# Add and layer norm: the fourth 16 rows loaded in two halves of 8, with the first store between the halves

## The chip, the cores and the metric

The kernel runs on one core of a Trainium2 chip. The metric is the time of one execution on the device, in microseconds (us).

## The reference

```python
# x, residual: (16, 1024, 512) float32; gamma, beta: 512; eps a number
z = x + residual
mean = np.mean(z, axis=-1, keepdims=True)
var  = np.var(z, axis=-1, keepdims=True)
return gamma * (z - mean) / np.sqrt(var + eps) + beta
```

There are 16,384 rows of 512 numbers. Each of the 128 partitions gets 128 rows. Whatever the kernel does, it must read 67.1 MB and write 33.6 MB.

## The kernel before

All large transfers go through one queue (the one of SP, the sync engine), in the order of a written plan. `x48+16` loads rows 48 to 63 of each partition from x, `r48+16` the same of the residual, `o0+16` stores the finished rows 0 to 15.

```python
PLAN = """
x0+8 r0+8 x8+8 r8+8 x16+16 r16+16 x32+16 r32+16
x48+16 r48+16 o0+16 r64+16 x64+16 o16+16 r80+16 x80+16
o32+16 r96+16 x96+8 x104+8 o48+16 r112+16 x112+8 x120+8
o64+16 o80+16 o96+16 o112+12 o124+4
"""
ADDS = [4, 4, 8] * 7 + [4] * 4          # rows of one add on POOL
Z_ROWS, R_ROWS = 64, 32                 # rings: rows of x (and result), of the residual
```

Before SP issues a transfer it waits for what that transfer needs, and while it waits nothing behind it in the plan is issued:

```python
    for kind, lo, n in moves:
        if kind == "x":        # the ring slot must have been stored
            while gone < len(stores) and stores[gone][0] < lo + n - Z_ROWS:
                nc.sync.wait_ge(so[gone], 16)
                gone += 1
            move(...)
        elif kind == "r":      # the ring slot must have been added
            wait_rows(s_add, "add", lo + n - R_ROWS)
            move(...)
        else:                  # the rows must be finished
            wait_rows(s_out, "out", lo + n)
            move(...)
```

So x64 waits until the store o0 has landed, r48 until 32 rows have been added, and o0 until 16 rows are finished. POOL (GpSimd) adds, ACT (ScalarE) takes the mean and the sum of squares of four rows at a time, DVE (VectorE) normalises in place:

```python
    for n in ADDS:                                    # POOL
        ...                                           # waits for the loads of these rows
        nc.gpsimd.tensor_tensor(out=z, in0=z, in1=part(rbuf, R_ROWS, lo, n), op=ALU.add
        ).then_inc(s_add, n)
    # ACT, per group of 4 rows (TURN), in a loop
            act.wait_ge(s_dve, due)
            act.wait_ge(s_add, due)
            ...
            for k in range(TURN):
                i = act.activation(out=junk_m[k][:, :], in_=zk[k], func=ACT.Identity,
                                   scale=-inv_d, accum_out=nm[j][:, k : k + 1])
            ...                                       # Square with accumulation, then Sqrt
```

## Time and profile before

| | |
|---|---|
| Time, median of the first 3 runs | 238.39 us (238.26 to 238.57) |
| Span of the profiled execution | 236.9 us |
| Bytes moved | 100.68 MB, 425 GB/s over the span |
| Busy share of the span | queue q1 99.2%, ACT 78%, DVE 75%, POOL 60% |

These lines are from the page of the kernel before: busy time of each engine, the DMA share in tenths in 40 slices of the span, and of the queues their packets, MB and the share of the time of all 16 DMA engines.

```profile
span 236.9 us, 1471 instructions
...
PE 3.7 (2%) x4; PEld 1.2 (0%) x4; DVE 177.2 (75%) x290; ACT 185.5 (78%) x545; POOL 143.0 (60%) x29
...
DMA  8999999999999999999999999999999999999996
...
q1 hardware_dynamic: 4176, 100.67, 99.2%
```

The 9s run from the first slice to the last but one: the DMA engines are at work all the time. No compute engine comes near.

The records of single DMA packets in the trace say at what rate. A packet here is what one partition moves in one transfer: 32 KB for 16 rows, 16 KB for 8. The usual packet of 32 KB takes 1213 ns, of 24 KB 912, of 16 KB 611, of 8 KB 309. Sixteen engines with 32,768 bytes each per 1213 ns make 432 GB/s, and 100.66 MB at that rate take 233 us. The span exceeds this by 3.9 us: the first packet starts at 1.0 us, the first ones are slow (up to 1465 ns for 16 KB), and the engines finish unevenly at the end.

The issue timeline of SP (start, length, engine, line, operation, transfer):

```profile
31.38 0.43 SPq L146 DMA_DIRECT2D zbuf<-in_x_dram  x1
59.41 0.33 SPq L146 DMA_DIRECT2D rbuf<-in_residual_dram  x1
59.78 0.43 SPq L146 DMA_DIRECT2D out_dram<-zbuf  x1
78.83 0.33 SPq L146 DMA_DIRECT2D rbuf<-in_residual_dram  x1
90.61 0.33 SPq L146 DMA_DIRECT2D zbuf<-in_x_dram  x1
90.98 0.43 SPq L146 DMA_DIRECT2D out_dram<-zbuf  x1
98.55 0.33 SPq L146 DMA_DIRECT2D rbuf<-in_residual_dram  x1
```

And the waits of the same queue in total (us, times, longest):

```profile
SPq L146 <- POOL zbuf L180: 94.0, 6, 27.6
SPq L146 <- DMA out_dram<-zbuf: 74.0, 4, 21.0
```

SP waits for 94 us on POOL and 74 us on stores. Set the issue times beside the landings: x64 is issued at 90.61, as soon as o0 has landed, but r64, issued at 78.83, lies ahead of it and lands at 99.97. I call that distance, 9.4 us, the margin of an issue.

### The profile page before, as it was taken

The page shows a single profiled execution, that of the slowest core. Times are in us where ns is not written, and L with a number is a line of the kernel's source. Part 1 is how long each engine was busy: PE and PEld are TensorE (multiplying, and loading weights), DVE is VectorE, ACT ScalarE, POOL GpSimd, SP SyncE. Part 2 cuts the span into 40 slices and gives each one's busy share as a digit, 9 for nine tenths or more (in the row PEclk, how much of TensorE's full clock was granted, in tenths as well). Part 3 has the DMA queues.
Part 4 walks back from the last instruction along what each step waited for, and adds up shares of the span by engine and source line. Part 5 has one row for each costly group of instructions (what it writes and reads, how often), then busy time and mean ns, then how long its engine had stood idle before and what let it go on. Part 6 is the DMA issues. An engine that isn't in the chain of part 4 may idle for free.

```text
span 236.9 us, 1471 instructions
## 1 busy us (share of the span) xinstructions
PE 3.7 (2%) x4; PEld 1.2 (0%) x4; DVE 177.2 (75%) x290; ACT 185.5 (78%) x545; POOL 143.0 (60%) x29
## 2 busy tenths in 40 slices
PE   0600000000000000000000000000000000000000
PEld 0100000000000000000000000000000000000000
DVE  0001977939699999999898989896989895698920
ACT  2019879497999999999999998979998956999300
POOL 0098920999799699604995059944995049950000
DMA  8999999999999999999999999999999999999996
GB/s 310 443 432 426 426 443 443 443 443 443 426 415 398 443 443 443 426 420 409 431 437 443 443 443 432 420 407 429 443 437 437 409 432 448 437 420 437 426 430 285
DMA packets 4181, 100.68 MB, mean 425 GB/s; under 512 B 466, under 2 KB 466, under 8 KB 468
## 3 DMA queue, kind: packets, MB, share of 16 engines
q1 hardware_dynamic: 4176, 100.67, 99.2%
q14 instruction: 1, 0.01, 0.0%
q10 hardware_dynamic: 4, 0.00, 0.0%
HBM read 67.11 MB, written 33.55 MB: 425 GB/s over the span
## 4 chain that ended last, share of the span: by engine, by line
DMA 71%; POOL 9%; ACT 9%; DVE 2%; issue 2%; SPq 1%; ACTq 0%; DVEq 0%; POOLq 0%
DMA out_dram<-zbuf 49%; DMA rbuf<-in_residual_dram 16%; POOL zbuf L180 9%; DMA zbuf<-in_x_dram 6%; ACT junk_s L212 5%; ACT junk_m L202 4%; SPq L146 1%; DVE zbuf L240 1%; DVE zbuf L252 1%; ACTq L202 0%; DVEq L240 0%; ACT std L221 0%; DVE rstd L249 0%; ACTq L193 0%; POOLq L177 0%
## 5 line engine op out<-in xcount | busy, mean ns | idle before, releaser
L180 POOL TENSOR_TENSOR zbuf<-zbuf,rbuf 128x2048 f32<-128x2048 f32 (+1 forms) x25 | 142.8, 5740 | 67.6 <-DMA zbuf<-in_x_dram 40.8
L240 DVE SCALAR_TENSOR_TENSOR zbuf<-zbuf,nm,gamma_p 128x512 f32 x128 | 87.1, 743 | 46.3 <-ACT junk_s L212 46.3
L202 ACT ACTIVATE junk_m<-zbuf 128x512 f32 x128 | 74.9, 585 | 29.1 <-POOL zbuf L180 27.5
L212 ACT ACTIVATE junk_s<-zbuf,nm 128x512 f32 x128 | 88.8, 694 | 1.0
L252 DVE SCALAR_TENSOR_TENSOR zbuf<-zbuf,rstd,beta_p 128x512 f32 x128 | 87.1, 743 | 1.1
L212 ACT ACTIVATION_READ_ACCUMULATOR junk_s<-zbuf,nm 128x1 f32 x128 | 23.9, 187 | 0.0
L202 ACT ACTIVATION_READ_ACCUMULATOR junk_m<-zbuf 128x1 f32 x128 | 23.9, 187 | 0.0
L221 ACT ACTIVATE std<-ssq,eps_t 128x4 f32<-128x4 f32 x32 | 9.5, 297 | 3.0
L249 DVE RECIPROCAL rstd<-std 128x4 f32<-128x4 f32 x32 | 5.5, 170 | 0.0
L190 ACT ACT_TABLE_LOAD x1 | 1.3, 1283 | 2.7 <-PEq L60 2.7
L132 PE MATMUL gamma_p<-gb_row,ones 1*128 1x512 f32 x2 | 2.0, 1119 | 7.2 <-DMA gb_row<-in_gamma_dram 7.2
L132 PE MATMUL beta_p<-gb_row,ones 1*128 1x512 f32 x2 | 1.9, 1052 | 0.0
L127 DVE MEMSET ones<- 1x128 f32 x1 | 0.2, 165 | 2.0 <-PEq L60 2.0
L132 PEld LDWEIGHTS beta_p<-gb_row,ones 1*128 1x128 f32 x2 | 0.7, 328 | 1.0 <-issue 0.5
L132 PEld LDWEIGHTS gamma_p<-gb_row,ones 1*128 1x128 f32 x2 | 0.5, 308 | 7.1 <-issue 7.1
L288 POOL MEMSET const-float32-0.0<- 128x1 f32 x1 | 0.1, 98 | 0.2 <-issue 0.2
L288 POOL MEMSET const-bfloat16-1.0<- 128x1 bf16 x1 | 0.1, 101 | 0.0
L288 POOL MEMSET const-uint8-127<- 128x1 uint8 x1 | 0.1, 101 | 0.0
L288 POOL MEMSET const-float32-1.0<- 128x1 f32 x1 | 0.1, 98 | 0.0
L128 DVE MEMSET eps_t<- 128x1 f32 x1 | 0.1, 59 | 0.0
## 6 DMA issues: line engine op xcount, KB each, us to landing
rbuf<-in_residual_dram SPq DMA_DIRECT2D x7, 4096.0 KB, 30.5
out_dram<-zbuf SPq DMA_DIRECT2D x7, 4096.0 KB, 28.6
zbuf<-in_x_dram SPq DMA_DIRECT2D x5, 4096.0 KB, 28.9
zbuf<-in_x_dram SPq DMA_DIRECT2D x6, 2048.0 KB, 14.9
rbuf<-in_residual_dram SPq DMA_DIRECT2D x2, 2048.0 KB, 15.7
out_dram<-zbuf SPq DMA_DIRECT2D x1, 3072.0 KB, 13.5
out_dram<-zbuf SPq DMA_DIRECT2D x1, 1024.0 KB, 10.2
gb_row<-in_gamma_dram ACTq DMA_DIRECT2D x1, 2.0 KB
```

The lines of the kernel that those rows point to most:

```text
L127: nc.vector.memset(ones[:, :], 1.0).then_inc(s_const, 1)
L132: nc.tensor.matmul(dest[:, :], ones[:, :], gb_row[:, k * D : (k + 1) * D], start=True, stop=True).then_inc(s_pe, 1)
L146: i = nc.sync.dma_start(out=out, in_=in_).then_inc(s, 16)
L180: nc.gpsimd.tensor_tensor(out=z, in0=z, in1=part(rbuf, R_ROWS, lo, n), op=ALU.add).then_inc(s_add, n)
L190: act.preload_act_table_set("sqrt_and_others")
L202: i = act.activation(out=junk_m[k][:, :], in_=zk[k], func=ACT.Identity, scale=-inv_d, accum_out=nm[j][:, k : k + 1],)
L212: i = act.activation(out=junk_s[k][:, :], in_=zk[k], func=ACT.Square, bias=nm[j][:, k : k + 1], accum_out=ssq[j][:, k : k + 1],)
L221: act.activation(out=std[j][:, :], in_=ssq[j][:, :], func=ACT.Sqrt, bias=eps_t[:, 0:1], scale=inv_d,).then_inc(s_std, TURN)
L240: dve.scalar_tensor_tensor(out=zk[k], in0=zk[k], scalar=nm[j][:, k : k + 1], in1=gamma_p[:, :], op0=ALU.add, op1=ALU.mult,)
L249: dve.reciprocal(out=rstd[j][:, :], in_=std[j][:, :]).then_inc(s_dve, TURN)
L252: i = dve.scalar_tensor_tensor(out=zk[k], in0=zk[k], scalar=rstd[j][:, k : k + 1], in1=beta_p[:, :], op0=ALU.mult, op1=ALU.add,)
L288: nc = _bacc.Bacc("TRN2", target_bir_lowering=False, num_devices=1)
```

## The change

Its intent, as far as the diff tells, is to bring the first store forward, so that its rows in the ring of x come free sooner, and to let POOL begin on half of the fourth 16 rows while the store runs.

```diff
-x48+16 r48+16 o0+16 r64+16 x64+16 o16+16 r80+16 x80+16
-o32+16 r96+16 x96+8 x104+8 o48+16 r112+16 x112+8 x120+8
-o64+16 o80+16 o96+16 o112+12 o124+4
+x48+8 r48+8 o0+16 x56+8 r56+8 r64+16 x64+16 o16+16
+r80+16 x80+16 o32+16 r96+16 x96+8 x104+8 o48+16 r112+16
+x112+8 x120+8 o64+16 o80+16 o96+16 o112+12 o124+4
```

Behind `r56+8` the two plans are the same.

## The prediction

> **What bounds the kernel now.** The DMA engines. The page gives 100.68 MB in a span of 236.9 us, 425 GB/s, and queue q1 busy for 99.2% of the 16 engines' span; ACT is busy 78%, DVE 75%, POOL 60%. In the packet records a 32 KB packet takes 1213 ns on its engine, so 16 engines move 432 GB/s; 100.66 MB at that rate is 233 us. The rest is 2.4 us before the first transfer is under way and about 1 us of small losses. The Trainium skill, "DMA: Bandwidth & Descriptors", section "Where 436 GB/s comes from", states a ceiling of 435 GB/s at the SBUF ports; this trace, at 432, agrees, so no order of moves can get much more out of the engines. Order matters only if the queue runs empty. It does not: over the span the engines were short of packets for 1.3 us in all, 0.2 at the start, 1.0 at the end.
>
> **What the change does.** Bytes stay the same. Two 4 MB loads become four of 2 MB, and the second halves go behind the first store. From the issue timeline and the order of the queue:
> - r48 needs 32 rows added (issued at 59.41 us); its first half needs only 24, so it issues near 50.5 us, and the first store right behind it near 51 instead of 59.78.
> - The first store runs from about 70.5 to 80.5 us instead of 80.5 to 90.6. The load x64, which waits for it, issues near 81 instead of 90.61, and the second store with it.
> - The second halves land near 85.5 and 90.4 us. POOL can add rows 48 to 55 at 78.8, but rows 56 to 63 only from 90.4 to about 99.3 (before: done at 98.5). r80 issues about 0.7 us later, with some 20 us of queue in front of it.
> - From about 90 us on, every transfer has its old place in the queue; the tail is the same.
>
> **Cost.** 16 KB packets take 611 ns against 1213 for 32 KB; two halves land 9.79 us apart against 9.71. Two split loads: about 0.15 us more. Two more issues (0.3 to 0.4 us of SP each) are off the path. A stretch of the last packets of r48 before the first store (up to 1678 ns instead of 1213, about 0.3 us once) should move to 68-70 us, not vanish.
>
> **On the critical path:** only the 0.15 us. The earlier store frees its rows 10 us sooner, but nothing on the path waited for them: the chain of waits follows the first store's landing at 90.6 only because the queue is always full.
>
> **Predicted:** 238.5 us, range 238.1 to 239.1 (8 in 10). Chances: faster by over 2% 0.01, within 2% 0.98, slower by over 2% 0.01.
>
> **What would show it right:** in the DMA view 8 loads of x and 4 of the residual of 2 MB (before 6 and 2), queue busy still about 99%; the first store landing near 80.5 us; the next store's issue near 81; r80's issue near 99.3; engine busy times unchanged; last store landing within 0.5 us of before.
>
> **What would make it wrong:** an empty stretch of the queue near 85 to 100 us, if POOL's later second half of the adds or the wait for the first store held back an issue over its 10 to 20 us of slack; or the stretched packets at the first turn from loads to stores growing, because the store now stands between two loads of half size. Gains could only come from that stretch vanishing, 0.3 us.

## The result

| | before | after |
|---|---|---|
| Median | 238.48 us (238.26 to 239.47, 6 runs) | 238.67 us (238.39 to 239.22, 6 runs) |
| Span of the profiled execution | 236.9 us | 237.1 us |

The ratio is 1.0005, with a 95% interval of 0.9985 to 1.0025: no difference. Ratios here are the mean time of one kernel's fast runs over that of the other's of the same rounds, so they are not quite the ratio of the medians quoted beside them.

The same lines of the page, after:

```profile
span 237.1 us, 1474 instructions
...
PE 3.7 (2%) x4; PEld 1.2 (0%) x4; DVE 177.2 (75%) x290; ACT 185.5 (78%) x545; POOL 143.1 (60%) x29
...
DMA  8999999999999999999999999999999999999997
...
q1 hardware_dynamic: 4464, 100.67, 99.3%
```

The 288 more packets are the two split loads (16 data packets more on each of 16 engines) and the completion records of two more transfers. The busy times of DVE and ACT are the same to a tenth, that of POOL to 0.1 us.

The issue timeline and the waits of SP, after:

```profile
31.37 0.43 SPq L146 DMA_DIRECT2D zbuf<-in_x_dram  x1
50.55 0.33 SPq L146 DMA_DIRECT2D rbuf<-in_residual_dram  x1
50.92 0.43 SPq L146 DMA_DIRECT2D out_dram<-zbuf  x1
51.40 0.43 SPq L146 DMA_DIRECT2D zbuf<-in_x_dram  x1
59.38 19.76 SPq L146 DMA_DIRECT2D rbuf<-in_residual_dram  x2
80.89 0.33 SPq L146 DMA_DIRECT2D zbuf<-in_x_dram  x1
81.27 0.43 SPq L146 DMA_DIRECT2D out_dram<-zbuf  x1
99.59 0.33 SPq L146 DMA_DIRECT2D rbuf<-in_residual_dram  x1
```

```profile
SPq L146 <- POOL zbuf L180: 103.7, 7, 26.7
SPq L146 <- DMA out_dram<-zbuf: 63.6, 4, 21.0
```

The first half of r48 is issued 8.9 us sooner than r48 was (50.55 against 59.41), the first store likewise, x64 and the second store 9.7 us sooner (80.89 against 90.61), and r80 1.0 us later (99.59 against 98.55). The waits moved by 10 us from stores to POOL. The last line of those above hides a second issue: r56 at 59.38 and r64 behind it at 78.82, as before.

The next table is worked out from the trace: issue of a transfer, the time at which its last engine reported, and the step since the landing before it.

```
         before                              after
      issue   landed    step             issue   landed    step
x48   31.38    70.53    9.71     x48+8   31.37    65.68    4.89
r48   59.41    80.52    9.99     r48+8   50.55    70.98    5.30
o0    59.78    90.59   10.07     o0      50.92    80.88    9.90
                                 x56+8   51.40    85.63    4.75
                                 r56+8   59.38    90.53    4.89
r64   78.83    99.97    9.39     r64     78.82   100.25    9.72
x64   90.61   109.69    9.72     x64     80.89   109.96    9.71
o16   90.98   119.62    9.93     o16     81.27   119.93    9.97
r80   98.55   129.09    9.47     r80     99.59   129.43    9.50
...
o124 226.67   236.89    2.49     o124   226.79   237.02    2.50
```

The issues moved by up to 10 us. From r64 on, no landing shown moved by more than 0.34 us; of those left out, that of o32 moved most, by 0.49 us (148.79 to 149.28).

The chain of waits shows the same (start, us, what; two pieces of it). Before:

```profile
59.78 30.81 DMA out_dram<-zbuf
...
90.98 28.65 DMA out_dram<-zbuf
```

After:

```profile
50.92 29.96 DMA out_dram<-zbuf
...
81.27 38.66 DMA out_dram<-zbuf
```

Each piece is a store, from its issue to its landing. The second store is issued 9.7 us sooner and takes 10.0 us longer: it only stands in the queue for longer. A chain that leads through a store says nothing of whether the store could have come sooner to any use.

### The profile page after: what moved, and what is told of

Read it like the earlier page. It is cut to its first block, busy times and chain, and to the rows that moved or that the text cites. A ratio compares the mean times of both kernels' runs of the same rounds, so it can differ in the third digit from the quotient of the medians.

```text
span 237.1 us, 1474 instructions
## 1 busy us (share of the span) xinstructions
PE 3.7 (2%) x4; PEld 1.2 (0%) x4; DVE 177.2 (75%) x290; ACT 185.5 (78%) x545; POOL 143.1 (60%) x29
## 3 DMA queue, kind: packets, MB, share of 16 engines
q1 hardware_dynamic: 4464, 100.67, 99.3%
## 4 chain that ended last, share of the span: by engine, by line
DMA 75%; ACT 9%; POOL 6%; DVE 2%; issue 2%; SPq 1%; ACTq 0%; DVEq 0%; POOLq 0%
DMA out_dram<-zbuf 53%; DMA rbuf<-in_residual_dram 16%; DMA zbuf<-in_x_dram 6%; POOL zbuf L180 6%; ACT junk_s L212 5%; ACT junk_m L202 4%; SPq L146 1%; DVE zbuf L240 1%; DVE zbuf L252 1%; ACTq L202 0%; DVEq L240 0%; ACT std L221 0%; DVE rstd L249 0%; ACTq L193 0%; POOLq L177 0%
```

## Experiments

All kernels below gave correct results except e7. The diffs show only the words of a line that matter; `...` marks what is left out.

Theory A: the queue is always full, so only bytes and, a little, packets count; the order matters only where the queue runs empty. Rival B: the earlier store gains something, and the split loads cost it again. Rival C: the chain of adds, ACT and DVE sets the time, and the change does not touch it.

### The change again, and each half of it alone

e1_after_again is the changed kernel, unedited, in five rounds.

> The changed kernel once more, for a tighter interval, beside the two halves of the change. Theory A (the queue of the DMA engines is always full, so only bytes and packets count): 0.1 to 0.25 us over before, ratio 1.0005 to 1.001. Rival B (the earlier store gains something that the split loads cost again): the same ratio here, told apart by the next two runs. Rival C (the chain of adds, ACT and DVE sets the time): ratio 1.000, nothing moved.

Measured: 238.66 us (238.39 to 239.05) against 238.36 before, ratio 1.0009, interval 0.9996 to 1.0022.

e2_split_only splits the loads and leaves the store behind all of them:

```diff
-x48+16 r48+16 o0+16 r64+16 x64+16
+x48+8 r48+8 x56+8 r56+8 o0+16 r64+16 x64+16
```

> The two loads split, all four halves still ahead of the first store. Theory A: the cost of the 16 KB packets alone, 0.15 us over before, and the first store landing at 90.6 to 90.9 us as before. Rival B: slower than the changed kernel by what the earlier store is worth, over 0.3 us. Rival C: no difference.

Measured: 238.40 us, ratio 1.0005, interval 0.9992 to 1.0018. The first store landed at 90.50 us. Three of the four halves landed 4.89 or 4.90 us after the transfer before; the fourth took 5.07, at the turn to the store.

e3_store_only moves the store and splits nothing:

```diff
-x48+16 r48+16 o0+16 r64+16 x64+16
+x48+16 o0+16 r48+16 r64+16 x64+16
```

> The first store ahead of the whole load of r48, no load split. Theory A: as before within 0.1 us, though the first store lands near 80.5 us and the second store and x64 issue near 81 us. Rival B: faster than before by over 0.3 us. Rival C: no difference. The stretched packets before the first store should be those of x48, near 67 to 70 us.

Measured: 238.38 us, ratio 1.0002, interval 0.9990 to 1.0014. The first store landed at 80.97 us and x64 was issued at 80.98, all as with the full change, and nothing was gained. What the split adds is seen here too. Without it POOL could add rows 48 to 63 only from 90.6 us on, after the whole of r48 had landed; r80 was issued at 108.53, 10 us later than before, and its margin was 11.3 us, against 21.1 before and 20.3 with the full change. That was still enough.

Rival B asked for e3 to be faster by over 0.3 us and for e2 to be slower than the full change; neither came. The medians of the three differ by less than 0.3 us, below what these runs resolve; a gain of 0.2 us or less would not have been seen.

e4_whole16 goes the other way and makes loads larger:

```diff
-x0+8 r0+8 x8+8 r8+8 x16+16 ...
+x0+16 r0+16 x16+16 ...
-... r96+16 x96+8 x104+8 o48+16 ...
+... r96+16 x96+16 o48+16 ...
```

> The opposite of splitting: the first 16 rows of x and of the residual, and x96, loaded whole. Theory A: 24 fewer packets on each engine, each worth about 9 ns, so 0.2 us under before, if the later first add (near 21.5 us instead of 12.3) leaves the queue full; the profile should show the queue never empty. Rival C: the first add comes 9 us later, so a chain of computing would end several us later.

Measured: 238.31 us, ratio 1.0008, interval 0.9990 to 1.0026. The 0.2 us were not to be seen: the spans are equal (236.9 us). The first add, though, came 10 us later, and that is what this run is good for. The timeline of POOL, of e4 and then of before:

```profile
22.22 17.77 POOL L180 TENSOR_TENSOR zbuf<-zbuf,rbuf 128x2048 f32<-128x2048 f32 x3 [21.78 <-DMA rbuf<-in_residual_dram]
```

```profile
12.33 8.95 POOL L180 TENSOR_TENSOR zbuf<-zbuf,rbuf 128x2048 f32<-128x2048 f32 x2 [11.90 <-DMA rbuf<-in_residual_dram]
```

A chain of computing that set the time would have ended later. It did not.

### Making the queue run empty

Theory A says when order would matter. e5_dry_one puts the first store behind the load of r64, so that x64, which waits for that store, has nothing queued ahead of it:

```diff
-o0+16 r64+16 x64+16
+r64+16 o0+16 x64+16
```

> The first store placed after the load of r64, so that the load of x64, which waits for that store to land, has nothing queued ahead of it: the queue must run empty once. Theory A: an empty stretch of 1.5 to 2.5 us near 100 us, in which no engine moves data, and that much more time in all: about 240.4 us. A theory that the order of moves does not matter at all: 238.4.

Measured: 243.15 us, ratio 1.0195: 4.8 us more, twice what I expected. e6_dry_four does it for the first four stores (r64, r80, r96 and r112 each ahead of its store).

> The same for each of the first four stores. Theory A: four empty stretches of 1.5 to 2.5 us, 6 to 10 us more, about 246.5 us. A theory that the order does not matter: 238.4.

Measured: 252.97 us, ratio 1.0606, 14.6 us more, where I had expected up to 10. The direction is A's, the size was wrong. The landings of e6, worked out as above (its later turns are left out), show why:

```
      issue   landed    step
r48   59.38    80.24    9.71
r64   78.82    92.05   11.81     issued 1.4 us before the load ahead of it landed
o0    79.19   101.78    9.73
x64  101.80   113.98   12.20     issued into an empty queue
r80  102.17   124.57   10.59     slow last packets, before the store
o16  102.64   134.30    9.73
x80  134.31   146.61   12.31     issued into an empty queue
```

I had missed two things. Moving r64 up made it late as well: it must wait for 48 rows to be added (78.8 us), and now only r48 lies ahead of it. A margin of 1.4 us was too little: the first packet of r64 started 0.96 us after its issue, at 79.77, no sooner than the last data of r48 ended (79.77), when the first engine had been done since 79.32, and the first packets took 1.8 to 2.2 us on 14 of the 16 engines. And after the engines have stood still together, the next turn from loads to a store costs 0.9 us: the last packet of 32 KB before it takes 1.8 to 2.3 us on every engine instead of 1.21. So e5 has two bad places, not one. (The profiled execution of e5 was its slowest, 244.5 us, so I take no durations from it; r64 was issued there at 78.91, with the same one load ahead.)

e10_dry_last was made to have one alone, late in the plan, with r112 well ahead of its turn:

```diff
-o48+16 r112+16 x112+8 x120+8
+r112+16 o48+16 x112+8 x120+8
```

> One dry place alone, where no other issue is late: the store of rows 48 to 63 goes behind the load of r112, so that x112, which waits for it, has nothing queued ahead. By e6_dry_four: 1.8 us without packets and 0.65 us of slow first packets, 2.45 us, and about 0.9 us more where the next load turns to a store with the engines in step. With that turn 241.5 us, without it 240.8 us. If e5_dry_one's 4.8 us were the price of one dry place: 243.2 us.

Measured: 241.33 us (241.29 to 241.51), ratio 1.0125, 3.1 us more: one empty place with its turn. The page's DMA share in 40 slices, the issues, and two stretches of 2 us (length; busy time and count on PE, PEld, DVE, ACT and POOL; clock; DMA share; GB/s), all of e10:

```profile
DMA  8999999999999999999999999999999599999997
...
q1 hardware_dynamic: 4176, 100.67, 98.6%
```

```profile
157.48 0.43 SPq L146 DMA_DIRECT2D out_dram<-zbuf  x1
187.75 0.80 SPq L146 DMA_DIRECT2D zbuf<-in_x_dram  x2
```

```profile
core 0: us, PE busy (x) PEld busy (x) DVE busy (x) ACT busy (x) POOL busy (x), PEclk, DMA share, GB/s
186.00:188.00 2.00, 0.00 (x0) 0.00 (x0) 1.06 (x3) 1.91 (x7) 0.00 (x0) 1.00 0.08 33
188.00:190.00 2.00, 0.00 (x0) 0.00 (x0) 2.00 (x5) 1.98 (x8) 0.00 (x0) 1.00 0.65 139
```

This view counts a packet in the stretch in which it starts, so 0.08 says that almost none started from 186 to 188 us; DVE and ACT went on working. The packet records give the hole itself, 1.43 us, and take it apart: the last data packet of the store ends at 187.28; the store is reported landed at 187.73 (0.45 us); SP issues x112 at 187.75; its first packet starts at 188.71 (0.96 us); and the first packets of 16 KB take about 1.3 us instead of 0.61.

### Fewer bytes, more computing

e7_half_bytes gives a wrong result. It loads half of r80, and adds what the ring held for the rest:

```diff
+            h = n // 2 if lo == 80 else n
-            move(part(rbuf, R_ROWS, lo, n), dram(rf, lo, n), ...)
+            move(part(rbuf, R_ROWS, lo, h), dram(rf, lo, h), ...)
```

> Wrong result on purpose: one load of the residual (r80) brings 8 of its 16 rows, all arithmetic and all waits as before. Theory A (bytes set the time): 2.1 MB at 432 GB/s less, 4.85 us, so 233.5 us. Rival C (the chain of computing sets it): unchanged, 238.4 us.

Measured: 233.35 us against 238.36, ratio 0.9785. Taking 2.1 MB away took away 5.0 us (4.85 expected), with all computing left in.

e8_act_more gives ACT one pass more per group of four rows:

```diff
+            act.activation(out=junk_s[0][:, :], in_=zk[0], func=ACT.Identity)
             for k in range(TURN):
                 i = act.activation(
```

> One more ACT pass over one row in each group of four rows, with its result thrown away: 32 more of about 0.6 us, 19 us more ACT work, ACT busy about 86%. Theory A: time within 0.2% of before, since the last stores still have some 5 us of queue ahead of them. Rival C: up to 19 us more.

Measured: 240.49 us, ratio 1.0085, 2.1 us more. That is a miss for my expectation (within 0.2%), though far from the 19 us that were the most under rival C. From the page of e8, and the stretches near its end:

```profile
PE 3.7 (2%) x4; PEld 1.2 (0%) x4; DVE 177.2 (74%) x290; ACT 202.1 (85%) x577; POOL 143.1 (60%) x29
...
q1 hardware_dynamic: 4176, 100.67, 98.3%
```

```profile
core 0: us, PE busy (x) PEld busy (x) DVE busy (x) ACT busy (x) POOL busy (x), PEclk, DMA share, GB/s
...
224.00:226.00 2.00, 0.00 (x0) 0.00 (x0) 1.97 (x5) 1.97 (x7) 0.00 (x0) 1.00 0.57 246
226.00:228.00 2.00, 0.00 (x0) 0.00 (x0) 1.33 (x3) 1.93 (x6) 0.00 (x0) 1.00 0.00 0
228.00:230.00 2.00, 0.00 (x0) 0.00 (x0) 1.93 (x3) 0.30 (x1) 0.00 (x0) 1.00 0.93 393
```

There was another hole. By the packet records no data moved from 226.58 to 228.18 us: the store o112 was issued at 227.35 (before: 220.88), after the store ahead of it had landed at 227.07. The margin in the kernel before was 6.2 us (220.88 against the landing of o96 at 227.13), and the issue came 6.5 us late. I had counted only the extra passes of the last groups, and not that ACT, busier all along, would enter the last 16 rows with a backlog: by the timeline it began its last four groups at 202.5 us, where before it began them at 197.4, right after their first add. If this reading is right, a delay of a few us must cost nothing (up to some 4.8 us by my estimate, the margin less the 0.45 and 0.96 us of e10). e9_act_half makes the extra pass in every second group only:

```diff
+            if j == 0:
+                act.activation(out=junk_s[0][:, :], in_=zk[0], func=ACT.Identity)
```

> Half of the extra ACT work of e8_act_more (one extra pass in every second group of four rows, 16 in all, about 8.3 us by the profile of that run). If e8 lost its 2.1 us only because its last stores were issued after the queue had emptied (o112 at 227.35 us, the store before it landed at 227.07), this run issues o112 before about 224 us and takes no more time than before, within 0.2%. If ACT sets the time in proportion to its work, half of e8's loss: 239.4 us.

Measured: 238.15 us against 238.22, ratio 0.9991, interval 0.9956 to 1.0026. o112 was issued at 221.77, only 0.9 us later than before, well inside its margin. The page:

```profile
span 236.7 us, 1487 instructions
...
PE 3.7 (2%) x4; PEld 1.2 (0%) x4; DVE 177.3 (75%) x290; ACT 193.9 (82%) x561; POOL 143.0 (60%) x29
...
q1 hardware_dynamic: 4176, 100.67, 99.4%
```

ACT worked 8.4 us more than before (193.9 against 185.5) and the kernel took no longer. In proportion to e8 it would have lost 1.05 us, and 239.4 is well above all four runs (237.98 to 238.28).

## Why the prediction was right

It said 238.5 us (238.1 to 239.1) and "within 2%" with 0.98; the median was 238.67.

- **The bound.** It named the DMA engines, at 432 GB/s by the packets. e7 shows it: 2.1 MB fewer, 5.0 us fewer. e9 shows the other side: 8.4 us more of ACT, no change. On the ceiling the Trainium skill ("DMA: Bandwidth & Descriptors", "Where 436 GB/s comes from") says 435 GB/s at the SBUF ports; the packets agree to 1%. The same skill, "HBM Reference", "Specifications (TRN2)", says that a core streaming alone measures about 425 GB/s, bounded by its 16 DMA engines; both profiles show 425 over the span. Which part of the path sets the limit, memory, ports or engines, no run here shows.
- **The moves.** The first half of r48 was predicted at 50.5 us and issued at 50.55, the store at 51 and 50.92, its landing at 80.5 and 80.88, x64 at 81 and 80.89, the landings of the second halves at 85.5 and 90.4 and at 85.63 and 90.53, r80 at 99.3 and 99.59. The last store landed 0.13 us later than before.
- **The critical path.** The earlier store bought margin, not time. x64 is now issued 19.4 us before the load ahead of it lands (80.89 against 100.25), where it was 9.4 before. Nothing used the first margin up, so a larger one is worth nothing. e3, the early store alone, shows this: 1.0002. The dry runs show what it would take for the store's place to matter: the margin must be used up, and then one place costs 2 to 3 us (two places 4.8 us in e5, one 3.1 us in e10, and 2.1 us in e8, where no turn to a store followed).
- **The cost of 0.15 us.** This stays below what the times can tell: e1's interval runs from 0.04% less to 0.22% more, and e2 is no clearer. Only the landings support it: halves that no turn disturbs come 4.89 us apart, so 19.56 for four against 19.42 for two whole loads. e4, which should have gained by the same arithmetic, showed no gain, so I do not call this term shown.
- **The stretched packets.** They moved from 77 to 79 us to 68 to 70 us, as said, and did not vanish: summed and divided by 16 engines, 0.38 us in either profile. Their size is not stable, though. It was 0.14 us in e2, about 0.6 in e3, and about 0.8 in the second profile of the changed kernel. So this one turn varies more than the cost that I predicted.

What stays open is why the first turn from loads to a store, and the turn after an empty place, are slow while the later turns give back in the next load what the store seemed to lose (9.93, then 9.47). That the engines are in step at the former is an argument, not shown. Nor is it shown why first packets after an empty place were slow for loads (1.26 us instead of 0.61 in e10) but not for the store in e8 (0.913 to 0.924 us instead of 0.912).

I found no version that beats the kernel before. Of the 3.9 us above the 233 us for the bytes, none was moved by a reordering here.

## What to carry to other kernels

Where one queue carries everything and is always full, judge a new order by the margins: the time between the issue of a transfer and the landing of what lies ahead of it. An issue that comes sooner gains nothing if its old margin was large enough (3.0 us was, for o124 in e8; 1.4 us was not, for r64 in e6), and a change that uses a margin up costs 2 to 3 us per place here, so long waits of the issuing engine and a chain of waits through stores are no proof of lost time. Look for holes in the DMA share by slice first, and when you slow an engine on purpose, count the backlog that it carries into the tail.

## What the Trainium skill lacked or had wrong

- "DMA: Bandwidth & Descriptors", "Anatomy of one DMA", gives about 2.0 us of fixed cost, from software-generated transfers, and puts most of it on the write receipt. For this hardware queue and one empty place (e10) the sum is alike, about 2.1 us, but the parts are not: 0.45 us from the last data packet to the reported landing (0.33 to 0.49 us at the empty places of e6 and e8), 0.96 us from issue to the first packet, and about 0.65 us of slow first packets. The page has no such account of the hardware queue.
- The same page, "Latency and other measured facts", gives about 600 ns to the first byte for this kind of queue. From the start of the issue to the start of the first packet it was 0.96 us in e10, 1.0 us at the start of the kernel and 0.83 us for the store in e8. From the end of the issuing instruction it was 0.64, 0.63 and 0.49 us, so the two agree for loads if the page counts from there; it does not say from where it counts.
- The same page, "Rules for kernel authors", asks for at least 1 MiB per transfer. It does not say how little size matters above that in a full queue: 2 MB loads landed 4.89 us apart (429 GB/s) and 4 MB loads 9.71 us (432 GB/s).
- No page read gives the time of a packet by its size, beyond a rate for one engine: 309, 611, 912 and 1213 ns for 8, 16, 24 and 32 KB in these traces (32 KB alike for loads and stores).
- No page read mentions the turn from loads to a store on one queue: next to nothing in the steady state, 0.14 to 0.8 us at the first turn, 0.9 to 1.1 us at the first turn after the queue had been empty.
